# Hybrid attention and state-space layer: V's tiles on another queue, earlier stores, and a new order in the last head pair

## The chip, the cores and the metric

The kernel runs on one core of a Trainium2 chip. The core has a matrix engine (TensorE, "PE" in the profile; its weight loads are "PEld"), a vector engine (VectorE, DVE), a scalar engine (ScalarE, ACT), a general engine (GpSimd, POOL) and SyncE (SP), which here only issues transfers. Transfers (DMAs) are issued on the queues of SyncE, ScalarE or GpSimd and are carried out by 16 DMA engines that all queues share. Each engine works through its own instructions in order and waits on semaphores for the others. The metric is device time in microseconds (us), the median of several runs.

## The reference, cut to what matters

One decoder layer over a sequence of 2048 tokens of width 1024, all in float32. The input projection makes q, k, v and a gate z for attention, and the inputs of a state-space mixer. Attention has 16 heads of width 64. Every head attends three times, with dilations 1, 4 and 16 and a window of 128 steps, and the three results are mixed by a softmax over their log-sum-exps:

```python
o1, l1 = dilated_window_attention(q, k, v, slopes, DILATIONS[0])
o2, l2 = dilated_window_attention(q, k, v, slopes, DILATIONS[1])
o3, l3 = dilated_window_attention(q, k, v, slopes, DILATIONS[2])
wts = jax.nn.softmax(jnp.stack([l1, l2, l3], axis=0), axis=0)
y_att = wts[0][..., None] * o1 + wts[1][..., None] * o2 + wts[2][..., None] * o3
y_att = rms_norm(y_att.reshape(Bsz, S, D_ATT) * silu(z_att), att_norm_g)
# y_ssm: state-space scan over chunks of 128, gated and normed in the same way
mix = jnp.concatenate([y_att, y_ssm], axis=-1)
x = layer_norm(alpha * x + jnp.einsum('bse,ed->bsd', mix, w_out), ln_g, ln_b)
```

## The kernel before, in words

The kernel has three stages. The first (up to about 1148 us) projects the input and runs the state-space scan; it leaves q, k, V, the gates, the scan's output (`d_us`) and the output weights, split into high and low parts (`d_wo`), in device memory. The change does not touch it.

**Attention** (1148 to 1613 us) goes over 8 pairs of heads (`pr`), in each over the three windows (`d` = 0, 1, 2: dilations 16, 4, 1 in the order of the tables), four groups of blocks (`qd`) and two halves (`half`): 24 units to a pair, listed in `todo` (L1251). In step `i` of the loop (L1256) the scores and exponentials of unit `i` are issued, the transposes of unit `i - 2`, and the products with V (`values`, L990) of unit `i - 3`. Everything else hangs on the position `at` = (d, qd, half) of that last unit. `manual_schedule` (L1255) keeps the order of the program on each engine named; the order between engines comes from semaphores alone. The next block starts a new such region (L1343), and the instructions of the two regions are merged by the compiler's own time model, which may put the head of the second into the tail of the first.

A tile is taken from a ring of a given number of buffers (`bufs`). Whoever takes the next tile waits until the last use of the tile that had that buffer. The rings that matter: `v` and `vs` (V, and V shifted by half a block) with 3 buffers each, `wb` with 3, `num` with 6, `ex` with 3, and one `q` and one `k` for each of two pairs in turn. In the last pair the same buffers are taken for output weights (`big`, L1133; `load_w`, L1137) and for split blocks (`free`).

While pair `pr` is in attention, pair `pr - 1` is combined. `statistics` (L1036) transposes minima and sums (L1041) in two parts, after the second and the third window, and stores them; `gather` (L1058) reads them back in another layout; `weights` (L1063) makes the three mixing weights and stores them (`d_wd`, L1081); `broadcast` (L1083) reads each weight back, spread over the partitions, into a `wb` tile, by two transfers on SyncE (L1089). A memset of one element before it (L1087) makes VectorE, too, wait until the buffer is free (not for the first weight, and not in the last pair). `combine` (L1099) runs steps 0 to 5 on GpSimd: the first weight times its result (L1111), the second (L1111), their sum (L1115), the third (L1111), the sum (L1115), times the gate z (L1125). The result `u` is a `wb` tile too, and `keep_u` (L1095, L1096) stores it to `d_ua`. So a pair takes five `wb` tiles (three weights, z, u) out of three buffers, and the tile of a pair's third weight takes the buffer that held `u` of the pair before it.

SyncE's order within a pair, as the program gives it: gather, V and shifted V of window 2 (L888) at (0,0,0), tables, the weights' store, first broadcast at (0,3,0), `keep_u` at (1,0,0), the other broadcasts at (1,0,1) and (1,2,0), tables, z at (2,0,0). GpSimd issues the next pair's q, k, V of windows 0 and 1 and shifted V of window 1 between the steps of `combine`.

**The output projection** (from 1613 us) takes blocks of 128 tokens. For a block and a branch (`br` = 1 for the scan, 0 for attention) the raw input is fetched (`fetch_raw`, L1150), split into high and low parts (`split`, L1159: a cast on ScalarE, L1167, and a difference, L1169), squared and summed for its norm (`squares`, L1172), and multiplied with eight weight tiles in two halves (`product`, L1191; 24 matmuls each). `residual` (L1179) fetches rows of the input, `scaled` (L1183) scales them, `add` (L1215, L1218) adds a product to them, and `norm` (L1220) finishes and stores them. Products take accumulators out of six in turn, four of them named `S`. The first eight products are those of branch 1 for blocks 0 to 3, as branch 0 needs the last pair, whose weights, broadcasts and `combine` (here on VectorE) run beside them. In the block before the change SyncE is not among the engines whose order is kept (L1343), and the time model orders it.

## Time and profile before

| | |
|---|---|
| median of three timed runs | 2011.88 us (2008.34 to 2013.04) |
| the profiled execution's own time | 2003.82 us |
| span of the profile | 2002.0 us |
| mean granted TensorE clock | 0.991 |
| PE busy | 1945.7 us (97%) |
| DVE, ACT, POOL busy | 1275.8, 1120.0, 998.3 us |
| DMA | 447.67 MB, mean 224 GB/s |

The profile is one execution, and its times are microseconds from the start of the span. A row of the order in time gives start, length, engine, line of the kernel, operation, the tile written and the tiles read, and in brackets how long the engine stood idle before and what released it. "SPq" and "ACTq" are transfers being issued by SyncE and ScalarE; "x4" means that several like instructions are merged into one row. A row of the busy time in stretches gives the stretch, its length, and for each engine busy time and number of instructions, then granted clock (1.00 is full), the mean busy share of the DMA engines and GB/s. A busy TensorE is not always at its peak, since matmuls overlap. L-numbers are lines of the kernel before.

### The profile page before, as it was taken

What the parts mean: (1) busy time and instruction counts of PE and PEld (TensorE: products, weight loads), DVE (VectorE), ACT (ScalarE), POOL (GpSimd) and SP (SyncE); (2) the same over time, 40 slices, a digit from 0 to 9 for tenths busy, and PEclk for the clock granted to TensorE, in tenths of its full rate; (3) what the DMA queues carried; (4) which work ended last, traced back from release to release, by engine and by line L of the source; (5) the groups of instructions that cost most, each with busy time, mean ns of one, the idle gap of its engine ahead of it and who ended that gap; (6) DMA issues with size and microseconds to landing.
All of it is one profiled execution on the core that took longest, in us unless ns stands there. A gap on an engine that the chain in (4) does not pass through costs nothing.

```text
span 2002.0 us, 42714 instructions
## 1 busy us (share of the span) xinstructions
PE 1945.7 (97%) x16008; PEld 1588.2 (79%) x16008; DVE 1275.8 (64%) x3204; ACT 1120.0 (56%) x3036; POOL 998.3 (50%) x877
## 2 busy tenths in 40 slices
PE   8999999999999999999999999999999888999998
PEld 7888899888888888988888877777777666888886
DVE  7655376887766655644454388888887736655553
ACT  5454343566556774456566488988888732322220
POOL 0366514666556667155565343676776622432221
PEclk9999999999999999999999999999999998999999
DMA  6788676566787876888888766888888988332210
GB/s 270 236 284 293 213 280 227 159 195 190 237 306 266 279 245 239 312 269 256 272 277 259 256 228 165 229 244 235 252 238 254 265 242 260 134 102 92 92 61 32
DMA packets 260656, 447.67 MB, mean 224 GB/s; under 512 B 44785, under 2 KB 146673, under 8 KB 249057
## 3 DMA queue, kind: packets, MB, share of 16 engines
q1 hardware_dynamic: 170912, 205.39, 32.2%
q0 software_dynamic: 39088, 142.54, 21.6%
q10 hardware_dynamic: 50448, 97.01, 15.7%
q8 instruction: 126, 2.06, 0.4%
q14 instruction: 82, 0.66, 0.1%
HBM read 301.85 MB, written 151.39 MB: 226 GB/s over the span
## 4 chain that ended last, share of the span: by engine, by line
PE 85%; DVE 5%; DMA 4%; ACT 3%; issue 2%; POOL 1%; SPq 0%; ACTq 0%; DVEq 0%; POOLq 0%
PE pp L260 13%; PE pp L264 13%; PE pp L262 13%; PE N L1002 7%; PE S L947 6%; PE T L976 5%; PE pp L309 4%; PE S L1201 4%; PE S L1203 4%; PE S L1202 3%; PE ss L309 2%; PE T L1201 2%; PE T L1203 2%; PE T L1202 2%; PE ss L627 2%
## 5 line engine op out<-in xcount | busy, mean ns | idle before, releaser
L217 POOL TENSOR_TENSOR w<-wr,w 128x512 fp32r<-128x512 f32 x217 | 285.6, 1327 | 268.2 <-ACT w L216 184.0
L962 ACT ACTIVATE P<-P,st 128x192 f32<-128x192 f32 (+1 forms) x768 | 323.4, 423 | 59.9 <-DVE st L953 55.4
L252 ACT COPY ev<-pp 128x512 f32<-128x512 f32 x200 | 117.1, 587 | 315.3 <-PE pp L264 281.5
L953 DVE CUSTOM_DVE_ANT_0 P<-S,tb 128x192 f32<-128x192 f32 (+1 forms) x768 | 205.8, 324 | 53.6 <-PE S L947 44.1
L272 DVE TENSOR_TENSOR ev<-pp,ev 128x512 f32<-128x512 f32 x152 | 101.2, 686 | 140.6 <-PE pp L264 95.9
L216 ACT CAST w<-wr 128x512 fp32r<-128x512 f32 x224 | 134.1, 620 | 23.5 <-DVE wr L211 11.9
L962 ACT ACTIVATION_READ_ACCUMULATOR P<-P,st 128x1 f32 x768 | 145.0, 189 | 0.0
L1111 POOL TENSOR_TENSOR wb<-num,wb 128x2048 f32<-128x2048 f32 x21 | 95.7, 4558 | 93.7 <-DMA wb<-d_wd 90.2
L978 DVE COPY PT<-T 128x512 f32<-128x512 f32 x192 | 131.7, 686 | 3.8 <-PE T L976 3.8
L976 PE MATMUL T<-ident,P 128*128 128x128 f32 x768 | 127.3, 288 | 6.7 <-DVE PT L978 4.5
L1002 PE MATMUL N<-PT,v 128*64 128x64 f32 (+1 forms) x1536 | 124.5, 259 | 4.2 <-DVE PT L978 3.5
L976 PEld LDWEIGHTS T<-ident,P 128*128 128x128 f32 x768 | 81.3, 141 | 52.9 <-ACT P L962 16.8
L211 DVE TENSOR_TENSOR wr<-wr 128x512 f32<-128x512 f32 x128 | 112.2, 877 | 9.3 <-DMA wr<-w 5.9
L947 PE MATMUL S<-k,ex 64*64 64x192 f32 (+1 forms) x2048 | 108.8, 322 | 3.2 <-issue 3.2
L1002 PEld LDWEIGHTS N<-PT,v 128*64 128x64 f32 x1536 | 79.4, 138 | 38.3 <-issue 22.7
L459 DVE SCALAR_TENSOR_TENSOR ss<-U,cw,ss 128x512 f32<-128x512 f32 x144 | 106.0, 752 | 2.9 <-ACT ss L455 0.6
L1177 DVE TENSOR_REDUCE tb<-P 128x128 f32<-128x1024 f32 x30 | 60.2, 2006 | 45.1 <-ACT P L1174 21.1
L1239 POOL TENSOR_TENSOR k<-k,wb 128x1024 f32<-128x1024 f32 x8 | 25.8, 3225 | 122.0 <-DVE k L1238 122.0
L587 ACT ACTIVATE mt<-csb,wdr 128x128 f32<-128x128 f32 x256 | 78.9, 395 | 0.9 <-PE ss L627 0.8
L947 PEld LDWEIGHTS S<-k,ex 64*64 64x64 f32 x2048 | 66.4, 134 | 15.4 <-issue 8.9
L596 DVE TENSOR_TENSOR mt<-mt,ss 128x1024 f32<-128x1024 f32 x32 | 39.0, 1220 | 54.1 <-ACT mt L592 53.7
L260 PE MATMUL pp<-TT4h,w 128*128 128x512 f32 x176 | 69.6, 395 | 0.0
(493 smaller groups left out, 5991.1 us busy)
## 6 DMA issues: line engine op xcount, KB each, us to landing
wr<-w ACTq DMA_DIRECT2D x164, 256.0 KB
d_wc<-w SPq DMA_DIRECT2D x48, 512.0 KB
w<-d_wc POOLq DMA_DIRECT2D x48, 512.0 KB, 6.4
wb<-d_wd SPq DMA_DIRECT2D x48, 512.0 KB
d_wo<-wot POOLq DMA_DIRECT2D x32, 512.0 KB, 4.3
csb<-d_cs ACTq DMA_DIRECT2D x32, 512.0 KB
d_wv<-w SPq DMA_DIRECT2D x14, 1024.0 KB
w<-d_wv POOLq DMA_DIRECT2D x14, 1024.0 KB, 8.7
```

What stands on the lines that cost most here:

```text
L216: nc.scalar.copy(h, r)
L217: low.tensor_tensor(l, r, h.bitcast(F32), op=OP.subtract)
L260: nc.tensor.matmul(ps, w[:, 0, k], th[:, k], start=start and k == 0, stop=False, skip_group_check=not start)
L262: nc.tensor.matmul(ps, w[:, 0, k], tl[:, k], start=False, stop=False, skip_group_check=not start)
L264: nc.tensor.matmul(ps, w[:, 1, k], th[:, k], start=False, stop=(k == 3), skip_group_check=not start)
L309: nc.tensor.matmul(o, (th, tl)[j == 1][:, k, t], w[:, int(j == 2), k], start=start and r % 2 == k == j == 0, stop=(k == 3 and j == 2), ski ...
L947: nc.tensor.matmul(o, A["q"][d][64 * h:64 * h + 64, blk, 64 * a:64 * a + 64], kv, start=True, stop=True)
L953: nc.vector.tensor_tensor_reduce(P[:, h, cs], sp[h][:, cs], t, -0.125, 3.0e38, OP.add, OP.min, accum_out=stat(A, 0, d, h, blk))
L962: nc.scalar.activation(p, p, AF.Exp, bias=stat(A, 0, d, h, blk), scale=-1.0, accum_out=stat(A, 1, d, h, blk))
L976: nc.tensor.transpose(tp[:, h, i], P[:, h, 256 * i:256 * i + 128], ident)
L978: nc.vector.tensor_copy(pt, tp)
L1002: nc.tensor.matmul(o, l, r, start=start, stop=True, skip_group_check=True)
```

## The change

In attention, V of window 1 (`load_v(pairs[pr], "v", 1)`) and shifted V of window 1 go from GpSimd's queue to SyncE's, at (0,0,0) of their own pair and (2,0,1) of the pair before; V of window 2 moves from (0,0,0) to (0,1,1), shifted V of window 2 to (1,1,1), V of window 0 from (1,2,0) to (2,0,0). `keep_u` moves from (1,0,0) to (0,0,1). In pair 7 the raw inputs of blocks 0 and 1 are fetched at (1,0,1) instead of (1,2,0), and block 0 is split at (1,2,0) to (1,3,0) instead of (2,0,1) and (2,1,0); output weights are loaded at other positions, ahead of the step of `combine` at the same position, and partly into other tiles; z of pair 7 is fetched in attention, on SyncE. The third weight of pair 7 is broadcast into a tile of V's ring. In the output block SyncE's order is kept too; the broadcasts of pair 7 are issued before the residuals, which move from ScalarE's queue to SyncE's together with `keep_u` of pair 6; the third and later steps (split of block 3, `combine`, `add`) are put into another order.

```diff
@@ -1082,7 +1082,8 @@
 
         def broadcast(A, d):
 
-            wb = A["w", d] = cm_.tile([128, NR, NJ], F32, name="wb", bufs=3)
+            pool, name = (io, "v") if A["pr"] == 7 and d == 2 else (cm_, "wb")
+            wb = A["w", d] = pool.tile([128, NR, NJ], F32, name=name, bufs=3)
             if d and A["pr"] < 7:
                 nc.vector.memset(wb[:, 0, 0:1], 0.0)
             for h in range(2):
@@ -1105,8 +1106,6 @@
             pu = lambda a: a.rearrange("p (n r j) -> p r n j", r=NR, j=8)
             if k in (0, 1, 3):
                 d = k - k // 2
-                if last:
-                    broadcast(A, d)
                 wb = A["wb"] = A.pop(("w", d))
                 eng.tensor_tensor(wb, A["num"][d], wb, op=OP.mult)
                 if k == 0:
@@ -1178,7 +1177,7 @@
 
         def residual(n):
             o = O[n] = os_[n // 2][:, n % 2 * D:n % 2 * D + D] if n < 4 else O.pop(n - 4)
-            (nc.scalar if n < 4 else nc.sync).dma_start(o, xc[n * 128:(n + 1) * 128, :])
+            nc.sync.dma_start(o, xc[n * 128:(n + 1) * 128, :])
 
         def scaled(n):
             nc.scalar.activation(O[n], O[n], AF.Copy, scale=ALPHA)
@@ -1243,11 +1242,11 @@
         O = {}
         pairs = {}
         STEPS = {(1, 0, 0): (0, "q", 1),
-                 (1, 1, 0): (1, "k", 1), (1, 2, 0): (2, "v", 1, 0), (1, 3, 0): (3, None, 0), (2, 0, 0): (None, "v", 1, 1),
-                 (2, 1, 0): (4, "vs", 1, 1), (2, 2, 0): (5, None, 0)}
-        LOADS = {(1, 0, 0): ((8, None, "k_0"),), (1, 1, 0): ((9, None, "q_0"),), (1, 2, 0): ((11, None, "vs"),),
-                 (1, 3, 0): ((12, 0, "q_1"), (13, 0, "v")), (2, 1, 0): ((10, None, "ex"),),
-                 (2, 2, 0): ((14, 0, "v"), (15, 0, "vs"))}
+                 (1, 1, 0): (1, "k", 1), (1, 2, 0): (2, None, 0), (1, 3, 0): (3, None, 0), (2, 0, 0): (None, "v", 1, 0),
+                 (2, 1, 0): (4, None, 0), (2, 2, 0): (5, None, 0)}
+        LOADS = {(1, 0, 0): ((8, None, "k_0"),), (1, 1, 0): ((9, None, "q_0"),),
+                 (1, 3, 0): ((12, 0, "q_1"), (13, 0, "v")), (2, 0, 0): ((11, None, "num"), (14, 0, "v"), (15, 0, "vs")),
+                 (2, 1, 0): ((10, None, "ex"),)}
         todo = [(pr, d, qd, half) for pr in range(8) for d in range(3) for qd in range(4) for half in range(2)]
         pts = {}
         TA = 2
@@ -1300,24 +1299,45 @@
                     if at == (0, 0, 0) and pr < 7:
                         pairs[pr + 1] = load_pair(pr + 1)
                     if at == (0, 0, 0) and pr:
+                        load_v(pairs[pr], "v", 1, nc.sync)
+                    if at == (0, 1, 1) and pr:
                         load_v(pairs[pr], "v", 2, nc.sync)
-                        load_v(pairs[pr], "vs", 2, nc.sync)
                     if pr and at == (0, 2, 0):
                         load_tab(pairs[pr], 2)
-                    if pr > 1 and at == (1, 0, 0):
+                    if pr > 1 and at == (0, 0, 1):
                         keep_u(pairs[pr - 2], nc.sync)
                     if pr and at in ((0, 2, 0), (0, 2, 1), (0, 3, 0)):
                         weights(pairs[pr - 1], 2 * qd + half - 4)
                     if pr and at in ((0, 3, 0), (1, 0, 1), (1, 2, 0)):
                         broadcast(pairs[pr - 1], d + (at == (1, 2, 0)))
+                    if pr and at == (1, 1, 1):
+                        load_v(pairs[pr], "vs", 2, nc.sync)
                     if pr < 7 and at == (1, 1, 1):
                         load_tab(pairs[pr + 1], 0)
                     if pr and at == (2, 0, 0):
                         load_z(pairs[pr - 1])
-                    if pr == 7 and at in ((2, 0, 1), (2, 1, 0)):
-                        split(0, 1, slice(4 * qd, 4 * qd + 4), (0,))
-                    if pr == 7 and at == (2, 1, 0):
-                        split(0, 1, parts=(1,))
+                    if pr < 7 and at == (2, 0, 1):
+                        load_v(pairs[pr + 1], "vs", 1, nc.sync)
+                    if pr == 7:
+                        if at == (1, 0, 1):
+                            X = big("ex", F32)
+                            for j in range(2):
+                                fetch_raw(j, 1, X[:, j * D:j * D + D])
+                        if at == (1, 2, 0):
+                            free.append(big("vs"))
+                        if at == (2, 0, 0):
+                            zt7 = cm_.tile([128, NR, NJ], F32, name="num", bufs=6)
+                            nc.sync.dma_start(f2(zt7), d_za[7])
+                        for e, hf, name in LOADS.get(at, ()):
+                            load_w(e, hf, name)
+                        if at == (2, 0, 0):
+                            free.append(big("num"))
+                        if at in ((1, 2, 0), (1, 2, 1)):
+                            split(0, 1, slice(4 * half, 4 * half + 4), (0,))
+                        if at == (1, 3, 0):
+                            split(0, 1, parts=(1,))
+                        if at in ((2, 2, 1), (2, 3, 0)):
+                            fetch_raw(qd, 1)
                     if at in STEPS:
                         k, x, nx, *dd = STEPS[at]
                         if pr and k is not None:
@@ -1329,23 +1349,11 @@
                                 load_x(pairs[pr + nx], x)
                     if at == (2, 2, 0) and pr < 7:
                         permute(pairs[pr + 1], 1)
-                    if pr < 7:
-                        continue
-                    for e, hf, name in LOADS.get(at, ()):
-                        load_w(e, hf, name)
-                    if at == (2, 0, 0):
-                        zt7 = cm_.tile([128, NR, NJ], F32, name="num", bufs=6)
-                        free += [big("num"), big("num")]
-                    if at == (1, 2, 0):
-                        X = big("ex", F32)
-                        for j in range(2):
-                            fetch_raw(j, 1, X[:, j * D:j * D + D])
-        with tc.manual_schedule(engines={E.PE, E.DVE, E.Activation, E.Pool}):
+        with tc.manual_schedule(engines={E.PE, E.DVE, E.Activation, E.Pool, E.SP}):
             A = pairs[7]
             small = stp.tile([128, 192], F32, name="st")
             os_.append(X)
             free.append(big("ex"))
-            fetch_raw(2, 1)
             squares(0, 1)
             split(1, 1)
             squares(1, 1)
@@ -1362,16 +1370,10 @@
                 ps = product(n, br, hf)
                 adds.append((n, br, hf, ps))
                 if i == 2:
+                    combine(A, 0)
+                    load_w(0, 0, "num")
                     for j in range(2):
                         scaled(j)
-                    add(*adds.pop(0))
-                    add(*adds.pop(0))
-                    for j in range(3):
-                        combine(A, j)
-                    load_w(0, 0, "num")
-                    fetch_raw(3, 1)
-                    residual(2)
-                    residual(3)
                 if i > 4:
                     while adds:
                         add(*adds.pop(0))
@@ -1385,32 +1387,42 @@
                             weights(A, n)
                         os_.insert(0, big("k_1", F32))
                         for n in range(2):
+                            broadcast(A, n)
+                        for n in range(2):
                             residual(n)
+                        broadcast(A, 2)
+                        keep_u(pairs[6], nc.sync)
+                        for n in range(2, 4):
+                            residual(n)
+                    if i == 3:
+                        combine(A, 1)
+                        load_w(1, 0, "num")
+                        combine(A, 2)
                     squares(*ops[j])
-                    if i == 0:
-                        keep_u(pairs[6], nc.scalar)
-                        nc.scalar.dma_start(f2(zt7), d_za[7])
                     for m in (j + 2,) if 4 < j < 30 else ():
                         fetch_raw(*ops[m])
                     if j >= 7 and j + 1 < 32 and ops[j + 1][1]:
                         residual(ops[j + 1][0])
                         scaled(ops[j + 1][0])
                 if i == 3:
-                    fetch_raw(0, 0)
+                    add(*adds.pop(0))
+                    add(*adds.pop(0))
                     for j in range(2, 4):
                         scaled(j)
+                    load_w(2, 0, "vs")
+                    fetch_raw(0, 0)
                     for j in range(3, 6):
                         combine(A, j)
                         if j < 5:
                             add(*adds.pop(0))
                 if i == 4:
-                    for e, name in enumerate(("num", "vs", "v", "wb", "num", "wb", "num")):
-                        load_w(1 + e, 0, name)
+                    for e, name in enumerate(("wb", "wb", "num", "wb", "num")):
+                        load_w(3 + e, 0, name)
                         if e == 2:
                             fetch_raw(1, 0)
                     for e in range(8):
                         load_w(e, 1)
-                    lgb = big("wb", F32)
+                    lgb = f2(A["acc"])
                     lg, lb = lgb[:, 0:D], lgb[:, D:2 * D]
                     nc.sync.dma_start(lg, dap(lng, 0, [[0, 128], [1, D]]))
                     nc.sync.dma_start(lb, dap(lnb, 0, [[0, 128], [1, D]]))
```

## The prediction

> **What bounds the kernel now.** I read the page first, then the busy time in stretches of the attention stage, then the waits, and the order of time around the longest ones.
>
> ```profile
> span 2002.0 us, 42714 instructions
> PE 1945.7 (97%) x16008; PEld 1588.2 (79%) x16008; DVE 1275.8 (64%) x3204; ACT 1120.0 (56%) x3036; POOL 998.3 (50%) x877
> ```
>
> TensorE is busy for 97% of the span; only 56 us are open, so a change of order can win only where TensorE waits or runs at a lower clock. The change touches two places: attention, pair by pair, and the passage into the output projection. Cut at the second statistics transpose of each pair (T below), the busy time in stretches gives pairs 1 to 7, then parts of single pairs, then the passage. The first number is the length, then busy time of PE, PEld, DVE, ACT, POOL, granted clock, DMA share, GB/s.
>
> ```profile
> 1211.04:1265.90 54.86, 53.39 (x1032) 40.18 (x1027) 46.74 (x240) 48.23 (x217) 32.52 (x19) 1.00 0.76 216
> 1265.90:1319.25 53.35, 53.06 (x1032) 40.02 (x1026) 46.57 (x240) 48.15 (x217) 35.20 (x30) 1.00 0.86 244
> 1319.25:1375.75 56.50, 53.29 (x1033) 39.98 (x1026) 47.12 (x240) 48.24 (x217) 39.86 (x32) 1.00 0.85 240
> 1375.75:1432.85 57.10, 53.75 (x1034) 40.15 (x1027) 47.30 (x240) 48.59 (x220) 40.55 (x32) 1.00 0.85 243
> 1432.85:1489.50 56.65, 53.72 (x1032) 40.12 (x1026) 47.13 (x239) 47.82 (x215) 40.50 (x32) 1.00 0.87 245
> 1489.50:1547.18 57.68, 55.61 (x1032) 41.30 (x1027) 46.96 (x240) 48.18 (x217) 40.85 (x33) 0.97 0.84 238
> 1547.18:1613.10 65.92, 58.45 (x988) 42.81 (x982) 49.98 (x218) 47.94 (x201) 46.84 (x34) 0.92 0.87 254
> ...
> 1265.90:1299.94 34.04, 33.75 (x613) 24.78 (x608) 30.38 (x161) 31.34 (x145) 15.95 (x21) 1.00 0.85 220
> 1547.18:1583.54 36.36, 34.32 (x614) 24.90 (x608) 30.86 (x161) 31.63 (x146) 18.82 (x22) 1.00 0.83 212
> 1583.54:1613.10 29.56, 24.13 (x381) 17.92 (x375) 19.12 (x58) 16.30 (x56) 28.02 (x13) 0.83 0.93 306
> ...
> 1613.10:1647.11 34.01, 32.85 (x151) 26.49 (x145) 7.41 (x16) 10.45 (x15) 3.68 (x5) 1.00 0.90 247
> 1647.11:1659.55 12.44, 0.40 (x2) 0.00 (x0) 7.71 (x4) 0.02 (x1) 4.51 (x7) 0.69 1.15 247
> 1659.55:1665.30 5.75, 5.75 (x14) 4.50 (x15) 4.68 (x3) 2.94 (x3) 0.35 (x2) 0.50 1.21 400
> ```
>
> The same work takes 53.35 us in pair 2 and 56.5 to 57.7 in pairs 3 to 6. Pair 7 takes 65.92. Then TensorE stands still for 12 us, and its next 5.75 us run at half clock.
>
> **Part A: products stored sooner, V on SyncE (pairs 1 to 6).** What lengthens pairs 3 to 7 is a wait on VectorE (waits of the attention stage; two rows of pair 7 in order of time).
>
> ```profile
> DVE wb L1087 <- DMA d_ua<-wb: 9.4, 4, 2.6
> ...
> 1576.76 0.06 DVE L1087 MEMSET wb<- 128x1 f32 x1 [2.44 <-DMA d_ua<-wb]
> ...
> 1577.21 0.41 ACT L962 ACTIVATE P<-P,st 128x128 f32<-128x128 f32 x1 [2.75 <-DVE st L953]
> ```
>
> The memset that opens the third weight's tile (`wb`) must wait until the product of two pairs before has left that tile, and behind it on VectorE stand the next scores; ScalarE then idles 2.75 us. Why it leaves so late is in SyncE's order (pair 7, T = 1547.18), with the product on GpSimd that needs the first weight:
>
> ```profile
> 1554.95 0.54 SPq L888 DMA_DIRECT2D v<-d_v  x1
> 1555.58 2.49 SPq L888 DMA_DIRECT2D vs<-d_v  x1
> ...
> 1562.02 0.36 SPq L1081 DMA_DIRECT2D d_wd<-cm  x1
> 1565.68 1.12 SPq L1089 DMA_DIRECT2D wb<-d_wd  x2
> 1566.86 0.58 SPq L1096 DMA_DIRECT2D d_ua<-wb  x1
> 1567.49 10.45 SPq L1089 DMA_DIRECT2D wb<-d_wd  x4
> ...
> 1573.15 4.53 POOL L1111 TENSOR_TENSOR wb<-num,wb 128x2048 f32<-128x2048 f32 x1 [11.16 <-DMA wb<-d_wd]
> ```
>
> The store (L1096) stands behind the weights' store and the first broadcast. Moved to (0,0,1) it goes out near 1555.5, 11 us sooner, and the memset at 1576.8 finds the tile free. That removes about 2.4 us from each of pairs 3 to 7.
>
> Against it stands what SyncE gets in exchange. Ahead of the weights' store it now carries V, product, V instead of V and shifted V, and shifted V for the third window goes behind the second broadcast. Rates from the DMA queues, SyncE's own row in 1557:1561 (V and shifted V alone) and 1567:1571 (broadcast alone), then GpSimd's and SyncE's rows in 1584:1587 (both at once); packets, MB, share:
>
> ```profile
> q1 hardware_dynamic: 2512, 1.28, 109.6%
> ...
> q1 hardware_dynamic: 133, 0.96, 106.0%
> ...
> q0 software_dynamic: 87, 0.71, 79.3%
> q1 hardware_dynamic: 79, 0.17, 34.4%
> ```
>
> V moves at 1.28/4 = 0.32 MB/us, a broadcast at 0.24. The exchange adds 1.05 + 1.05 - 0.98 = 1.1 MB, 3.5 us; I take back 1 us because shifted V no longer moves while the statistics are gathered (bounds 0 and 2, no row has it). So the first weight lands 2.5 us later than now (1573.15, T + 26.0), at T + 28.5; the second 1.05/0.24 = 4.4 later, T + 32.9; shifted V 0.98/0.32 = 3.1 later, T + 36.0. It is first read one unit (2.4 us, 19.3/8 from the second part of pair 2, which is 53.35 - 34.04) after the first part: T + 34.0 + 2.4 = T + 36.4. It fits, by 0.4 us. The other V tiles have more room, but the first one for the next pair is put behind one more product on GpSimd:
>
> ```profile
> 1533.68 2.63 POOL L886 DMA_DIRECT2D v<-d_v  x4
> ```
>
> It is issued by 1536.3; the 4.5 of one product later is 1540.8, and a transfer of this size takes 7.5 from issue to use (1565.68 to 1573.15): it lands about 1 us after T of the next pair (1547.18), where its first readers come within one unit of 2.4. In a shorter pair that is tight too. I take 54.4 us for each of pairs 1 to 6, the 53.35 of pair 2 and one us of such waits (bounds 53.35 and 56.5). Pairs 3 to 6: 227.9 to 217.6; pairs 1 and 2: 108.2 to 108.8. **A = -9.7.**
>
> [...]
>
> **Part B: pair 7.** The first block's raw input is now asked for at (1,0,1), behind both broadcasts, and ScalarE's first cast of it stands at (1,2,0). That cast is due just before the exponentials quoted above, 1577.21 - 2.75 = 1574.5. The raw tile can't land before the second broadcast, T + 32.9 = 1580.1, and 0.8 us more (its first 0.26 MB at 0.32): ScalarE waits 6.4 us, with the next exponentials and the copies that free TensorE's accumulators behind it. I count 6 us for TensorE, and 2 for a lower clock after it (a wait of 3.2 us costs more below). Worse is possible: the first output weights (1 MB) now go ahead of the first product on GpSimd and meet V and the weights' store, and where both queues run they share by packets (87 to 79), so large packets push SyncE's small ones back, by up to 1.05/0.24 = 4.4 us. Better is possible if ScalarE has slack: none lost. First part: 34.0 + 8 = 42 for 36.4, +5.6 (bounds -2.4 and +11.6).
>
> [...]
>
> In the second part the split on GpSimd, which held TensorE, goes away:
>
> ```profile
> 1600.26 0.50 PE L1203 MATMUL S<-k,num 128*128 128x512 f32 x1 [3.23 <-POOL num L1169]
> ...
> 1600.26:1610.50 10.24, 8.75 (x90) 6.37 (x92) 8.54 (x8) 5.98 (x15) 10.22 (x4) 0.52 0.75 243
> ```
>
> That is 3.2 us and then 8.75 x 0.48 = 4.2 of clock. Reductions and the second block's split still fall in here, so of 7.4 I take 5.5 (bounds 2 and 9). **B = +5.6 - 5.5 = +0.1.**
>
> **Part C: the passage.** Now (SyncE's wait, then order of time on the engines):
>
> ```profile
> SPq L1089 <- DMA d_wd<-cm: 11.8, 2, 8.6
> ...
> 1624.60 0.38 SPq L1081 DMA_DIRECT2D d_wd<-cm  x1
> ...
> 1634.79 1.06 ACT L1184 ACTIVATE k<-k 128x1024 f32<-128x1024 f32 x1
> ...
> 1646.81 2.29 DVE L1111 TENSOR_TENSOR wb<-num,wb 128x2048 f32<-128x2048 f32 x1 [9.23 <-DMA wb<-d_wd]
> ...
> 1658.28 1.22 DVE L1169 TENSOR_TENSOR num<-P,num 128x1024 fp32r<-128x1024 f32 x1
> 1660.62 1.99 DVE L1177 TENSOR_REDUCE tb<-P 128x128 f32<-128x1024 f32 x1 [1.12 <-ACT P L1174]
> ...
> 1664.74 0.74 DVE L1218 SCALAR_TENSOR_TENSOR ex<-S,st,ex 128x512 f32<-128x512 f32 x1
> ```
>
> The weights' store takes 9.0 us until the broadcasts start (1624.60 plus 0.38 plus 8.6), because ScalarE's queue sends residuals, the product and z beside it; two products then stand ahead of the third block's split (L1169), for which TensorE waits. With ScalarE's queue empty I give the store 4.5 us (3.7 in pair 7 above, 1562.02 to 1565.68; 9 if the output weights on GpSimd alone do it): 1629.1. First weight 7.5 later, 1636.6; second 1641.0; two residuals, 1.05 MB at 0.32, 1644.3. ScalarE scales both before it casts the third block, three times about 1.0: 1647.3. Split 1.2, two more products' steps 4.6, reduction 2.0: 1655.1; the first add 0.7: 1655.8. That last step is what is late next: the split is done by 1648.5, but the seventh product needs an accumulator that only the first add frees, and that add has been moved behind the products. TensorE resumes at 1655.8 for 1659.55. The half clock stays. **C = -3.8** (bounds -9 and 0). After that the output weights arrive no later than TensorE asks, as now.
>
> **At nothing** I cost the rest: other tiles for output weights (they are asked for no later), z of pair 7 read during attention (1 MB less in the passage, already in C as an empty ScalarE queue), the third weight in V's ring (no wait for the product to leave), and SyncE's order written out to the end. The last hides here:
>
> ```profile
> 1673.35:2002.00 328.65, 318.93 (x1401) 258.49 (x1399) 179.10 (x242) 78.68 (x112) 89.33 (x36) 0.99 0.30 99
> ```
>
> The DMA engines are at 0.30, and a block's raw input is asked for two blocks ahead. If a store of output rows held SyncE for longer than that, each late load would cost its lateness.
>
> Sum: -9.7 + 0.1 - 3.8 = -13.4. The profiled run took 2003.8, so 1990.4; the three timed runs have a median of 2011.9, 8 us above that run, and I carry the difference over: **1998.5 us**. About 0.2% (4 us) is what a measurement of this kernel can tell from no change.
>
> **The rivals.**
> 1. *The last pair runs clean*: the raw input lands in time for the cast. For it: TensorE is up to two units ahead of ScalarE's due work. Against it: both broadcasts are ahead in one queue. B is 8 better: 1990.5. Chance 0.15.
> 2. *V waits replace the memset's wait*: shifted V or the first V comes 2 us late, pairs stay at 56. A is near 0, so -3.7: 2008.2, no change to tell. For it: 0.4 us of room. 0.14.
> 3. *Slower: shifted V behind the second broadcast.* Each us that it lands late holds TensorE that long in each of seven pairs; from 13.4/7 = 1.9 us late the change loses. At 3 us late it is +7.6, 2019.5, more with a lower clock, as pair 6 shows 0.97. For it: GpSimd's loads share by packets. Against it: the next load there starts only after the first product, 4.5 us past the first weight. 0.12.
> 4. *The passage doesn't change*, since the store stays at 9 us beside the output weights: C is 0, 2002.3. 0.09.
> The forecast has 0.50 and its own range is 1990 to 2007.
>
> **How the numbers follow.** Forecast, rival 1 and rival 4 are faster: 0.74. Same 0.14, slower 0.12. The range runs from 1988 (rival 1 and a little) to 2013, which leaves out rival 3 and the ends of others.
>
> **What would show it.** A: no row of L1087 waiting for d_ua, pairs 3 to 6 at 53.5 to 55; wrong if L1002 waits for V. B: a wait of ScalarE's L1167 for ex<-d_us near T + 27, and no wait of L1203 for GpSimd's L1169. C: L1089 less than 5 us after L1081, TensorE waiting for L1218 rather than L1169. The forecast falls if pairs 3 to 6 stay over 56 us.

## The result, and the profile after

The changed kernel takes 2021.5 us (median of 7 runs, 2016.1 to 2030.9), the kernel before beside it 2007.6 (7 runs). The ratio is 1.0074, with a 95% interval of 1.0048 to 1.0100: slower, where 1998.5 was forecast and 2013 was the end of the range. In the profiled execution the span went from 2002.0 to 2017.3 us, and TensorE is as busy in share as before:

```profile
span 2017.3 us, 42713 instructions
PE 1950.2 (97%) x16008; PEld 1592.5 (79%) x16008; DVE 1273.4 (63%) x3204; ACT 1118.9 (55%) x3036; POOL 980.6 (49%) x863
```

The busy time in stretches says where the 15.3 us are. Before the change: pairs 1 to 6 together, and the rest after the last statistics transpose (columns as in the prediction; the two parts of pair 7 stand there).

```profile
1211.04:1547.18 336.14, 322.81 (x6162) 241.75 (x6157) 281.83 (x1435) 289.21 (x1297) 229.48 (x173) 0.99 0.84 238
...
1613.11:2002.00 388.89, 365.96 (x1598) 296.02 (x1593) 205.79 (x272) 93.18 (x131) 101.42 (x53) 0.98 0.40 124
```

After: pairs 1 to 6, first and second part of pair 7, the rest.

```profile
1208.52:1557.10 348.58, 328.24 (x6163) 245.88 (x6157) 280.14 (x1435) 289.43 (x1297) 217.52 (x162) 0.98 0.83 232
1557.10:1602.57 45.47, 36.38 (x612) 26.71 (x607) 30.80 (x161) 32.67 (x148) 24.38 (x23) 0.89 0.85 237
1602.57:1635.41 32.84, 26.29 (x394) 20.14 (x391) 18.37 (x57) 15.03 (x53) 20.13 (x11) 0.84 0.72 235
1635.41:2017.30 381.89, 362.01 (x1584) 292.85 (x1579) 207.59 (x272) 93.77 (x131) 101.01 (x53) 0.98 0.38 122
```

Pairs 1 to 6 lost 12.4 us, pair 7 lost 9.1 and 3.3, the rest won 7.0, and the stage began 2.5 us sooner in this execution: +15.3. In pairs 1 to 6 TensorE's idle time grew by 7.0 us (13.3 to 20.3) and its busy time by 5.4, at a clock of 0.98 for 0.99. By pair the loss isn't where the stall was: pairs 1 and 2 took 59.4 and 57.9 us (54.9 and 53.4 before), pairs 3 to 6 57.3 to 58.5 (56.5 to 57.7 before). No single pair can be read closely, though: pair 1, in which no product is stored yet, took 54.9 us in e1 and 58.1 in e4, two runs below whose programs are alike in it.

TensorE's waits in pairs 1 to 6 (sum, times, longest), before:

```profile
PE T L976 <- DVE PT L978: 4.3, 3, 1.7
PE N L1002 <- DVE PT L978: 3.5, 3, 1.7
PE S L947 <- issue: 2.1, 3, 1.4
...
PE T L976 <- ACT P L962: 0.8, 1, 0.8
PE T L976 <- ACT num L1030: 0.8, 1, 0.8
```

and after:

```profile
PE N L1002 <- issue: 8.9, 7, 2.7
PE S L947 <- issue: 7.4, 5, 2.1
PE T L976 <- ACT P L962: 3.0, 2, 1.6
```

The waits for VectorE are gone but for 0.9 us of short ones. In their place stands "issue": time in which TensorE waited for nothing that the profile shows. That became the question of the experiments.

Not all of the waits for VectorE before the change stood behind the memset. Two pairs of rows, each VectorE's wait and the one of TensorE behind it:

```profile
1330.52 0.39 DVE L1069 TENSOR_TENSOR mm<-cm 128x32 f32<-128x32 f32 x1 [1.34 <-DMA cm<-d_st]
1333.06 0.68 PE L1002 MATMUL N<-PT,v 128*64 128x128 f32 x8 [1.69 <-DVE PT L978]
...
1406.63 0.06 DVE L1087 MEMSET wb<- 128x1 f32 x1 [2.42 <-DMA d_ua<-wb]
1408.56 0.63 PE L976 MATMUL T<-ident,P 128*128 128x128 f32 x4 [1.74 <-DVE PT L978]
```

The 3.5 us of L1002 stand behind VectorE's wait for the gathered statistics (L1069). Behind the memset stand the 4.3 us of L976, one wait in each of pairs 3 to 5; behind the memset of pair 6 (2.6 us at 1519.35) TensorE has no wait for VectorE; it had just waited 1.4 us put down to "issue". So VectorE's 2.4 us cost TensorE 1.2 to 1.7.

In pair 7 and the passage, ScalarE in order of time:

```profile
1593.89 0.62 ACT L1166 CAST vs<-ex 128x512 fp32r<-128x512 f32 x1 [9.73 <-DMA ex<-d_us]
...
1606.60 1.06 ACT L1173 ACTIVATE ex<-ex 128x1024 f32<-128x1024 f32 x1 [4.68 <-POOL vs L1168]
```

TensorE:

```profile
1596.47 0.48 PE L1002 MATMUL N<-PT,v 128*64 128x64 f32 x4 [9.09 <-ACT num L1030]
...
1608.68 0.69 PE L984 MATMUL T<-ident,P 128*128 128x128 f32 x2 [4.38 <-ACT sT L1046]
...
1626.03 0.44 PE L984 MATMUL T<-ident,P 128*128 128x128 f32 x2 [2.17 <-DVE PC L987]
...
1676.13 0.77 PE L1200 MATMUL S<-k,vs 128*128 128x512 f32 x1 [10.92 <-DVE k L1217]
```

SyncE:

```profile
1572.99 0.48 SPq L1081 DMA_DIRECT2D d_wd<-cm  x1
1580.11 2.41 SPq L1090 DMA_DIRECT2D wb<-d_wd  x4
1582.56 2.02 SPq L1154 DMA_DIRECT2D ex<-d_us  x4
...
1646.05 0.38 SPq L1081 DMA_DIRECT2D d_wd<-cm  x1
1650.41 3.17 SPq L1090 DMA_DIRECT2D wb<-d_wd  x4
1653.69 1.22 SPq L1180 DMA_DIRECT2D k<-xc  x2
```

GpSimd:

```profile
1587.43 4.49 POOL L1110 TENSOR_TENSOR wb<-num,wb 128x2048 f32<-128x2048 f32 x1 [15.20 <-DMA wb<-d_wd]
...
1604.22 2.35 POOL L1168 TENSOR_TENSOR vs<-ex,vs 128x1024 fp32r<-128x1024 f32 x1
```

ScalarE's cast waits 9.7 us for the raw input, and TensorE 9.1 behind it. Later ScalarE's squares (L1173) wait 4.7 us for the split on GpSimd (L1168), and TensorE 4.4 behind them. In the passage TensorE waits once, 10.9 us, for the first add (L1217) and no more for the split of block 3. Beside each of the four gaps in its rows its clock stands at 0.50, for 10.2, 6.8, 3.4 and 13.7 us in that order; the first of these two stretches holds such time and time at full clock:

```profile
1596.00:1608.00 12.00, 7.82 (x107) 5.82 (x107) 4.03 (x19) 6.23 (x24) 11.45 (x6) 0.64 1.07 286
...
1608.68:1612.00 3.32, 3.32 (x38) 2.49 (x38) 0.42 (x1) 1.83 (x8) 3.32 (x2) 0.50 0.10 17
```

### The profile page after: what moved, and what is told of

Its sections match the earlier page's. It is cut to its first block, busy times and chain, and to the rows that moved or that the text cites. A ratio compares the mean times of both kernels' runs of the same rounds, so it can differ in the third digit from the quotient of the medians.

```text
span 2017.3 us, 42713 instructions
## 1 busy us (share of the span) xinstructions
PE 1950.2 (97%) x16008; PEld 1592.5 (79%) x16008; DVE 1273.4 (63%) x3204; ACT 1118.9 (55%) x3036; POOL 980.6 (49%) x863
## 4 chain that ended last, share of the span: by engine, by line
PE 89%; DVE 3%; DMA 3%; ACT 2%; issue 2%; POOL 0%; SPq 0%; ACTq 0%; DVEq 0%; POOLq 0%
PE pp L260 14%; PE pp L264 14%; PE pp L262 14%; PE N L1002 8%; PE S L947 6%; PE T L976 5%; PE pp L309 4%; PE S L1200 4%; PE S L1201 4%; PE S L1202 4%; PE ss L309 2%; PE T L1200 2%; PE T L1201 2%; PE T L1202 2%; PE ss L627 2%
## 5 line engine op out<-in xcount | busy, mean ns | idle before, releaser
L1002 PE MATMUL N<-PT,v 128*64 128x64 f32 (+1 forms) x1536 | 125.2, 260 | 9.6 <-ACT num L1030 9.1
L976 PE MATMUL T<-ident,P 128*128 128x128 f32 x768 | 128.9, 291 | 3.0 <-ACT P L962 3.0
L976 PEld LDWEIGHTS T<-ident,P 128*128 128x128 f32 x768 | 82.4, 143 | 49.9 <-issue 18.8
L1002 PEld LDWEIGHTS N<-PT,v 128*64 128x64 f32 x1536 | 79.9, 139 | 43.4 <-issue 23.2
L1238 POOL TENSOR_TENSOR k<-k,v 128x1024 f32<-128x1024 f32 x8 | 25.8, 3220 | 122.5 <-DVE k L1237 122.5
L1176 DVE TENSOR_REDUCE tb<-P 128x128 f32<-128x1024 f32 x30 | 60.0, 1999 | 37.9 <-ACT P L1173 25.3
```

The source lines that it names most:

```text
L976: nc.tensor.transpose(tp[:, h, i], P[:, h, 256 * i:256 * i + 128], ident)
L1002: nc.tensor.matmul(o, l, r, start=start, stop=True, skip_group_check=True)
```

## The experiments

All runs in one table: ratio to the kernel before, timed beside it; length of pairs 1 to 6 in the profiled execution; TensorE's waits in them put down to "issue" and all others (some of the others turn out to be of the same kind, see "What 'issue' is"). Six pairs at the 53.35 us of pair 2 before would be 320.

| run | ratio (95% interval) | pairs 1-6 | issue | other |
|---|---|---|---|---|
| before | 1 | 336.1 | 2.6 | 10.5 |
| changed kernel | 1.0074 (1.0048 to 1.0100) | 348.6 | 16.3 | 3.9 |
| e1 sooner store alone | 1.0024 (1.0012 to 1.0036) | 349.9 | 15.4 | 2.1 |
| e2 V's moves alone | 1.0047 (1.0030 to 1.0064) | 355.4 | 6.4 | 15.8 |
| e4 changed, V back | 1.0070 (1.0055 to 1.0085) | 345.0 | 13.1 | 4.4 |
| e5 e4, early split back | 1.0049 (1.0031 to 1.0067) | 347.4 | 13.0 | 5.5 |
| e6 e1, broadcasts in 2 KB rows | 1.0065 (1.0048 to 1.0082) | 345.6 | 0.5 | 18.1 |
| e7 before, broadcasts in 2 KB rows | 1.0105 (1.0077 to 1.0133) | 353.9 | 1.2 | 21.5 |
| e8 before, 2 MB more, 8 KB rows | 1.0031 (1.0014 to 1.0049) | 344.8 | 8.1 | 10.8 |
| e9 before, 2 MB more, 2 KB rows | 1.0042 (1.0029 to 1.0056) | 351.5 | 12.3 | 11.0 |
| e10 e1, 3 MB less | 0.9976 (0.9961 to 0.9991) | 341.3 | 14.2 | 1.5 |
| e13 before, 3 MB less | 0.9931 (0.9905 to 0.9958) | 333.3 | 4.9 | 5.6 |
| e11 passage alone | 0.9981 (0.9967 to 0.9995) | 339.0 | 3.3 | 10.8 |
| e12 before without memset | 0.9985 (0.9975 to 0.9996) | 340.8 | 6.4 | 7.1 |
| e14 e1, third broadcast later | 1.0020 (1.0010 to 1.0029) | 347.9 | 17.5 | 3.3 |
| e15 e11 without memset | 0.9972 (0.9959 to 0.9985) | 342.4 | 9.8 | 8.1 |
| e16 e6, k ahead | 1.0031 (1.0012 to 1.0050) | 349.0 | 8.3 | 13.0 |
| e17 e16 with passage | 1.0009 (0.9997 to 1.0022) | 345.2 | 4.0 | 10.3 |
| e18 e17 in 4 KB rows | 0.9966 (0.9954 to 0.9978) | 340.3 | 7.4 | 7.0 |
| e19 e18, old store, no memset | 0.9960 (0.9947 to 0.9972) | 341.9 | 11.0 | 6.8 |

One profiled execution can stand a few us from the median of its kernel (e8's took 2008.5 us, its median is 2013.1); the ratio decides.

### Parts of the change (e1, e2, e4, e5)

The sooner store alone:

```diff
-                    if pr > 1 and at == (1, 0, 0):
+                    if pr > 1 and at == (0, 0, 1):
                         keep_u(pairs[pr - 2], nc.sync)
```

> The kernel before with one edit: the product's store (keep_u) at (0,0,1) instead of (1,0,0). Theory F (the loss in pairs 1 to 6 comes from V in SyncE's queue, which makes TensorE wait for its own instructions): the store alone removes the memset's wait of about 2.4 us in pairs 3 to 7, so 8 to 12 us faster than before, and the gaps of TensorE that the profile puts down to 'issue' stay as few as before (3.5 us in the waits of L947). Rival M (a TensorE that doesn't stop at the memset simply runs out of instructions later, whatever V does): within 2 us of before, with 'issue' gaps of 7 us or more in L947 and L1002. Rival L (V itself is late): as F, since V is untouched.

2011.6 us, 1.0024. The stall that the prediction wanted gone is gone, and the kernel is slower. Rival M comes nearest: "issue" takes 15.4 us in pairs 1 to 6, as in the changed kernel, with V untouched. Its time is missed: 4.6 us slower, where M had at most 2. Theory F, that V's place in SyncE's queue does it, falls.

V's moves alone (as in the change's diff, the store at its old place):

> The kernel before with V's five moves alone (V and shifted V of window 1 on SyncE, V of window 2 at (0,1,1), shifted V of window 2 at (1,1,1), V of window 0 at (2,0,0)); the product's store stays at (1,0,0). Theory F: pairs 1 and 2 lose 4 to 5 us each, as in the changed kernel, with gaps put down to 'issue'; pairs 3 to 6 keep the memset's wait and lose 3 or more each as well: 12 to 30 us slower than before. Rival L: the same sign, but then TensorE's L1002 waits for a DMA of v or vs in the profile. Rival M: within 4 us of before, because the memset's wait still covers it.

2018.8 us, 1.0047, slower as theory F and rival L had it; M, with at most 4 us, is missed again. Here shifted V did come late, which is rival L. TensorE's waits in pairs 1 to 6:

```profile
PE N L1002 <- DMA vs<-d_v: 12.6, 5, 3.0
PE N L1002 <- issue: 5.0, 4, 1.6
```

This is the prediction's third rival, at the 3 us it named, but only with the old store. In the changed kernel the store has left the place ahead of shifted V, and no row of L1002 waits for a DMA.

The changed kernel with V's moves undone:

> The changed kernel with V's five moves undone (sooner store, last pair and passage as changed). Theory F: pairs 1 to 6 take 53.5 to 55 us each, 12 + 10 us less than in the changed kernel; pair 7 still waits for the raw input, perhaps 3 us less as a MB less stands ahead of it: 1993 to 2003, which is 5 to 15 us faster than before. Rival M: pairs 1 to 6 stay at 57 to 58 us and the time at 2015 to 2021.

2022.3 us, 1.0070, just above what M had. V's moves are worth nothing in the changed kernel, which ends F a second time.

Then also the early split of block 0 undone:

```diff
-                        if at == (1, 0, 1):
+                        if at == (1, 2, 0):
                             X = big("ex", F32)
...
-                        if at in ((1, 2, 0), (1, 2, 1)):
-                            split(0, 1, slice(4 * half, 4 * half + 4), (0,))
-                        if at == (1, 3, 0):
+                        if at in ((2, 0, 1), (2, 1, 0)):
+                            split(0, 1, slice(4 * qd, 4 * qd + 4), (0,))
+                        if at == (2, 1, 0):
                             split(0, 1, parts=(1,))
```

> As the run with V's moves undone, and in the last pair the raw input is asked for at (1,2,0) and block 0 is split at (2,0,1) and (2,1,0), as before the change. Compared with that run it prices the early split. If the cast that waits for the raw input is what lengthens the first part of pair 7 (by 9.1 us in the changed kernel) and the split on GpSimd what holds the second part, the first part goes back to 34 to 37 us, the second stays at 29 to 33: 6 to 10 us faster than with the early split, about 1990 to 1995. If the first part stays over 42 us, the late first broadcast or the lower clock is the cause and the times agree within 3 us.

2017.3 us, 1.0049, far from the 1990 to 1995 that were expected. The parts of pair 7, with the early split (e4):

```profile
1555.56:1603.09 47.53, 36.11 (x614) 26.29 (x608) 31.10 (x161) 32.66 (x148) 26.79 (x25) 0.89 0.90 230
1603.09:1637.42 34.33, 27.23 (x396) 20.65 (x390) 18.32 (x57) 15.02 (x53) 20.59 (x11) 0.85 0.66 220
```

and without it (e5):

```profile
1557.16:1593.53 36.37, 34.08 (x614) 24.80 (x608) 30.96 (x161) 31.71 (x146) 16.15 (x22) 1.00 0.79 214
1593.53:1635.56 42.03, 28.73 (x397) 21.83 (x391) 19.14 (x58) 16.18 (x55) 31.74 (x14) 0.80 0.78 254
```

The cast costs the first part 11.2 us, as thought. But the second part then takes 42.0 us, not 29 to 33. SyncE and TensorE there:

```profile
1610.33 22.34 SPq L1154 DMA_DIRECT2D P<-d_us  x4
```

```profile
1616.61 0.80 PE L1202 MATMUL S<-k,vs 128*128 128x512 f32 x1 [6.34 <-POOL vs L1168]
...
1625.79 0.79 PE L1200 MATMUL S<-ex,vs 128*128 128x512 f32 x1 [4.09 <-DMA ex<-d_wo]
```

TensorE waits 6.3 us for the same split on GpSimd, and 4.1 for an output weight. SyncE spends 22 us over the raw inputs of blocks 2 and 3, which are asked for at (2,2,1) and (2,3,0), while exponentials still use their ring. The statistics' store stands behind them but isn't held: they are done at 1632.7, before its transpose at 1635.6.

### What "issue" is

Two queues of the trace carry instructions. One of them, q8, moves 126 packets of 16,384 bytes in the kernel before and in the changed one (the other has packets of 8,192 bytes and less). TensorE has 32,405 instruction records (matmuls, weight loads and 389 of its sequencer), which fits packets of 256 instructions (126 x 16,384 / 32,405 = 63.7 bytes each). In e1 SyncE's queue is alone for 8.2 us:

```profile
q1 hardware_dynamic: 526, 1.83, 105.3%
```

In the 1.5 us after that an instruction packet moves:

```profile
q1 hardware_dynamic: 36, 0.19, 63.5%
q0 software_dynamic: 12, 0.10, 30.6%
q8 instruction: 1, 0.02, 5.6%
q14 instruction: 1, 0.01, 3.0%
```

and then TensorE goes on:

```profile
1476.42 0.28 PE L1002 MATMUL N<-PC,vs 64*64 64x64 f32 x4 [3.26 <-issue]
```

This holds for all 125 gaps of TensorE of 0.7 us or more, between 1205 and 1605 us, that are put down to "issue" in the kernel before, the changed one and the eighteen of the experiments (e6 has none): each ends 2.2 to 3.1 us after the start of a q8 packet. The 108 such gaps with another releaser end anywhere from 0.1 to 10 us after one.

TensorE's own count says it more sharply. If its records are numbered in the order of their start, the last one before each of the 125 gaps is number 193 past a multiple of 256. Of the 108 others, 86 stand elsewhere, and 22 stand at number 193 too: these are most likely waits for instructions that the profile puts down to another engine. The two waits of L976 for ScalarE in the rows after the change are among them, as are the two in the rows before. Counted in this way, waits for instructions in pairs 1 to 6 went from 4.2 us (before) to 19.3 (changed), 16.9 in e1, and all other waits from 8.9 to 0.9, 0.6 in e1.

Counting gives the delay as well: outside attention a packet mostly starts when TensorE has run some 155 records past a multiple of 256. From there to number 193 of the next 256 are 294 records, an estimated 7.6 us at the pace of pair 2 (53.35 us for 2058 matmuls and weight loads). As 2.2 to 3.1 us pass between a packet's start and TensorE's going on, one that starts some 5 us behind that point would, by this estimate, leave TensorE dry; the packets behind the 125 gaps started 4.4 to 9.7 us behind it. The mean of this delay in us, in pairs 1 to 7, in their parts (a packet belongs to the part in which it starts), and outside (before 1148 us and after pair 7):

```
                          attention  first parts  second parts  outside
before                         3.72         3.54          3.98     1.92
changed kernel                 4.21         4.02          4.40     1.90
e1 sooner store                4.31         4.21          4.43     1.89
e6 e1, rows of 2 KB            3.05         2.22          4.43     1.82
e7 before, rows of 2 KB        2.54         2.37          2.76     1.86
e8 before, 2 MB more, 8 KB     4.22         3.88          4.71     1.84
e9 before, 2 MB more, 2 KB     4.64         4.10          5.39     1.82
e10 e1, 3 MB less              3.62         3.69          3.55     1.80
e13 before, 3 MB less          3.27         2.68          3.92     1.89
```

Packets start later in attention than outside it (before 3.72 us for 1.92, changed 4.21 for 1.90). The reading that fits is that TensorE there often stands close to the end of the instructions that it has, and runs dry when a packet starts late. Six runs change the traffic.

Broadcasts in rows of 2 KB, on top of the sooner store (e6) and on the kernel before (e7):

```diff
             for h in range(2):
-                nc.sync.dma_start(f2(wb[64 * h:64 * h + 64]), dap(d_wd[A["pr"]], (d * 2 + h) * S, [[0, 64], [1, S]]))
+                for c in range(0, S, 512):
+                    nc.sync.dma_start(f2(wb[64 * h:64 * h + 64])[:, c:c + 512],
+                                      dap(d_wd[A["pr"]], (d * 2 + h) * S + c, [[0, 64], [1, 512]]))
```

> The kernel with the sooner store alone, and each broadcast read in rows of 2 KB (four transfers of a quarter of the columns for one) instead of 8 KB; same bytes, same queue, same place. Theory P (TensorE's instructions come in packets of 16 KB over the same DMA engines, and packets of 8 KB of SyncE's queue keep such a packet waiting until TensorE runs dry): the gaps of TensorE that the profile puts down to 'issue' shrink below half of the 4 to 6 us a pair that they and their neighbours cost now, pairs 2 to 6 take 53.5 to 56 us instead of 58 to 60, and the time is 1992 to 2002. Rival S (it is the bytes in flight, not the size of a packet): no change against the sooner store alone, 2009 to 2014. Rival X (the gaps have nothing to do with the DMA engines): no change either, and no relation of gaps to instruction packets.

> The kernel before with the broadcasts in rows of 2 KB and nothing else. Theory P: the memset's wait of 2.4 us in pairs 3 to 7 stays, the 'issue' gaps of pairs 1, 6 and 7 go: 3 to 10 us faster than before, 1997 to 2004. Rivals S and X: within 2 us of before, or slower where eight transfers for two hold SyncE longer.

2021.7 us (1.0065) and 2029.7 (1.0105): the times went against theory P. The gaps did what it said: "issue" falls from 15.4 to 0.5 us (e6), the delay in first parts from 4.2 to 2.2, and pairs 1 to 6 win 4 us on e1 in the profiled execution, not the some 20 that the theory wanted of pairs 2 to 6. TensorE's longest waits there are now others:

```profile
PE S L947 <- DMA k<-d_k: 13.3, 5, 3.6
PE N L1002 <- DVE PT L978: 3.5, 3, 1.7
```

The sixteen transfers of two broadcasts hold SyncE for 11 to 13 us instead of 2.4 (in pairs 2 to 6), the weights land later, and GpSimd, which waits for them, asks for the next pair's k behind the second step. The rows are smaller and also spread over a longer time; these runs don't tell the two apart.

Two MB more in the third window, which nobody waits for, in rows of 8 KB (e8; e9 has rows of 2 KB, a quarter of the columns at a time):

```diff
+    d_xx = [dtile(f"d_xx{i}", [128, 2, S]) for i in range(8)]
...
                         load_z(pairs[pr - 1])
+                    if 0 < pr < 7 and at in ((2, 0, 1), (2, 1, 1)):
+                        for c in range(0, S, 2048):
+                            nc.sync.dma_start(dap(d_xx[pr], qd * S + c, [[2 * S, 128], [1, 2048]]),
+                                              dap(d_za[pr - 1], c, [[S, 128], [1, 2048]]))
```

> The kernel before with 2 MB more on SyncE in the third window of pairs 1 to 6 (two copies of 1 MB from device memory to device memory in rows of 8 KB at (2,0,1) and (2,1,1)), which no instruction waits for. Theory P: TensorE gets new 'issue' gaps in the third window, and each of pairs 1 to 6 takes 1.5 to 4 us more: 2016 to 2031. Rival X: TensorE waits for nothing that these copies delay, within 2 us of before. Rival S: as P.

> As the run with 2 MB more in rows of 8 KB, but the same bytes in rows of 2 KB. Theory P: most of the loss is gone, within 4 us of before. Rival S: as slow as with rows of 8 KB, 2016 to 2031. Rival X: within 2 us of before, as with rows of 8 KB.

2013.1 us (1.0031) and 2017.2 (1.0042). Rival X is out: transfers that nobody waits for cost time, and "issue" goes from 2.6 to 8.1 and 12.3 us, with packets later than before (3.7 to 4.2 and 4.6). Theory P had the signs but too much for 8 KB rows (2016 us or more). And rows of 2 KB were no better here, so the size of a row alone isn't the rule; this is what rival S had, though in e6 and e7 the delay fell with the bytes unchanged, which S doesn't explain.

Three MB a pair less, with the sooner store (e10) and on the kernel before (e13):

```diff
         def load_v(A, x, d, queue=nc.gpsimd):
 
+            if A["pr"] and (x, d) != ("v", 0) and (x, d) != ("vs", 1):
+                A[x][d] = A[x][0 if x == "v" else 1]
+                return
```

> The kernel with the sooner store alone, with V of windows 1 and 2 and shifted V of window 2 not loaded in pairs 1 to 7 (3 MB of the some 13 MB that a pair moves): the products of these windows read V of window 0 and shifted V of window 1 instead, so part of the attention's result is another one, with the same instructions on TensorE. Theory D (in attention the DMA engines are the bound: TensorE's own instruction packets are one of the things that come late behind other transfers, and with a stall taken away another transfer is late): the sooner store now keeps its gain, pairs 1 to 6 take 53.3 to 54.5 us each, gaps put down to 'issue' under 1 us a pair, 1975 to 1990. Rival X (TensorE's gaps have another cause than the DMA engines): pairs stay at 57 to 60 us, 2006 to 2014.

> The kernel before with the same 3 MB a pair left out (same remark on the result). Theory D: the memset's wait stays in part, since the first broadcast and the store behind it go out sooner too: pairs 3 to 6 take 53.5 to 56 us, 1978 to 1996, between 0 and 10 us slower than with the sooner store. Rival X: 2003 to 2011.

2002.3 us (0.9976) and 1993.7 (0.9931): 9.3 and 12.7 us less than the same kernels with the traffic. Less traffic helps, but less than theory D said: with the sooner store "issue" is still 14.2 us, though packets start no later on average (3.6 us) than in the kernel before (3.7). And the sooner store still loses, 8.5 us here.

### The memset, the store's place, and the passage (e11, e12, e14, e15)

The kernel before without the memset, store at its old place:

```diff
-            if d and A["pr"] < 7:
-                nc.vector.memset(wb[:, 0, 0:1], 0.0)
```

> The kernel before without the memset that opens the second and third weight's tile (L1087); the product's store stays at (1,0,0), so that the third broadcast's transfer itself, in SyncE's queue, waits until the product has left its buffer. Theory B (the sooner store loses because the three broadcasts, 3 MB in rows of 8 KB, then run without a break and hold TensorE's instruction packets back): here the store still stands between the first two broadcasts and the third still starts late, so the stall of VectorE goes and nothing comes in its place: pairs 3 to 6 take 54 to 56 us, 1996 to 2003. Theory K (any stall taken away is paid back, since TensorE only runs dry of instructions sooner): within 3 us of before, 2003 to 2010, or slower.

2004.1 us against 2008.1, 0.9985. The stall is worth about 3 us (interval 0.8 to 5.0), not 2.4 us in each of five pairs. Its profiled execution doesn't show where they were won: pairs 1 to 6 took 340.8 us in it, for 336.1 before. Of TensorE's waits for VectorE, those of L976 behind the memset (4.3 us) are gone; what is left stands behind the wait for the gathered statistics. "Issue" grows:

```profile
PE N L1002 <- DVE PT L978: 4.1, 3, 2.0
PE N L1002 <- issue: 3.7, 3, 1.9
PE S L947 <- issue: 2.7, 3, 1.3
```

The sooner store with the third broadcast at (1,3,0) instead of (1,2,0):

> The kernel with the sooner store alone, and the third broadcast at (1,3,0) instead of (1,2,0), some 5 us later. Theory B: the burst of broadcasts is broken, gaps put down to 'issue' near the start of the third window fall, pairs 2 to 6 take 55 to 57 us instead of 58 to 60, and the time is 1997 to 2005. Theory K: no change against the sooner store alone, 2008 to 2015.

2010.6 us, 1.0020: no change against e1. Theory B in this form falls, and theory K (what is taken away is paid back) stands: it had e12 at 2003 to 2010 us and allowed the 3.

The passage alone: the block after attention, `broadcast` and `residual` as in the changed kernel, attention as before, and

```diff
+            fetch_raw(2, 1)
+            fetch_raw(3, 1)
             squares(0, 1)
...
                         for n in range(2, 4):
                             residual(n)
+                        nc.sync.dma_start(f2(zt7), d_za[7])
```

> The kernel before with the passage of the changed kernel alone: attention in its old order (V, store, early raw input and split all as before), in the output block SyncE's order kept, broadcasts ahead of the residuals, the third broadcast in V's ring, residuals on SyncE, split of block 3 ahead of the second product; blocks 2 and 3 are fetched at the head of the block and z behind the residuals. If the passage's gain (some 7 us from the last statistics transpose to the end) stands by itself: 1998 to 2004, 3 to 9 us faster than before, and rest after that transpose 380 to 384 us. If the gain is only time that pair 7 lost before it: within 2 us of before.

2003.2 us, 0.9981 (0.9967 to 0.9995): faster than before, by 3 to 4 us. The rest takes 382.6 us, and the second part of pair 7 30.1, as before the change: the loss in pair 7 doesn't belong to the passage. Without the memset as well:

> The passage of the changed kernel alone (run before this one at 0.9981 of before), without the memset. The sum of the two: by theory B 1992 to 1999, by theory K 1999 to 2007.

2002.1 us, 0.9972, what theory K had for the two together (1999 to 2007).

### Repairs (e16 to e19)

k ahead of the second step, broadcasts in 2 KB rows (pair 7's in 8 KB):

```diff
                         k, x, nx, *dd = STEPS[at]
+                        if x == "k" and 0 < pr < 7:
+                            load_x(pairs[pr + nx], x)
                         if pr and k is not None:
                             combine(pairs[pr - 1], k)
...
-                            else:
+                            elif x == "q" or not pr:
                                 load_x(pairs[pr + nx], x)
```

> As the run with the sooner store and broadcasts in rows of 2 KB, with two edits: the next pair's k is asked for on GpSimd ahead of the second step of the combination instead of behind it (4.5 us sooner), and the broadcasts of the last pair, in the passage, stay in rows of 8 KB. Theory P2 (rows of 2 KB let TensorE's instructions through, and what they gained in the first two windows was lost because the slower broadcasts hold GpSimd, and so k, by up to 3.6 us a pair): the waits for k go, no gaps put down to 'issue' come back, pairs 2 to 6 take 54 to 57 us, 2003 to 2010, 5 to 14 us faster than without the two edits. Theory K (what is taken away comes back elsewhere): pairs stay at 57 to 61 us, 2010 to 2022.

> The same with the passage of the changed kernel. The passage was worth 4 us by itself: by theory P2 1997 to 2006, by theory K 2005 to 2018.

> The same with broadcasts in rows of 4 KB: half the transfers on SyncE, so the weights land sooner than with 2 KB. If the delay of an instruction packet goes with the size of the rows, 'issue' gaps come back in part (up to half of the 3 us a pair with 8 KB), 1998 to 2008; if any row below 8 KB is as good, it is 2 to 5 us faster than with 2 KB.

> The last kernel (passage, rows of 4 KB, k ahead) with the product's store at its old place (1,0,0) and without the memset. It prices the store's place where instruction packets are delayed less. If the old place is better by itself, as the run without the memset was 7.5 us faster than the one with the sooner store: 1993 to 1998. If that difference came from rows of 8 KB running without a break, it is gone with rows of 4 KB: 1998 to 2004.

2014.3 (1.0031), 2010.1 (1.0009), 2000.3 (0.9966) and 2001.9 (0.9960, against a 2010.3 beside it). The wait for k went, and the two edits of e16 together win some 7 us on e6, as theory P2 had it; but the time stays above the 2010 us it allowed, and "issue" came back in part. Rows of 4 KB are some 10 us better than rows of 2 KB: 2000.3 us is inside what was expected if the delay goes with the size of the rows (1998 to 2008), and above the 2 to 5 us expected if any row below 8 KB is as good. Whether the sooner weights or something else brings the 10 us was not taken apart. With 4 KB rows the new place of the store, and the old place without the memset, give the same within the intervals. e18 and e19 beat both kernels, by 0.34% and 0.40% of the kernel before.

## Why the prediction was wrong

**A, the step that failed: "That removes about 2.4 us from each of pairs 3 to 7."** The wait of the memset is gone, the store goes out where it was put, and no V is late in pairs 1 to 6, all as worked out. A came out at +12.4 for -9.7 even so, for two reasons.

VectorE's 2.4 us were not TensorE's. Behind them TensorE lost 4.3 us in pairs 3 to 5 together and nothing in pair 6, so the memset's wait had not much over 4 us to give. e12, which takes this wait away without moving anything, wins about 3 us.

And the stall sat on top of another limit, which the prediction didn't price: the packets of q8, read as TensorE's own instructions. Where TensorE doesn't stop for VectorE it would use its instructions up sooner, and stop for the next packet. That its stops go with these packets is shown (125 gaps at one place of its count, each ending 2.2 to 3.1 us after a packet's start); that it stops for want of one, and that the missing stall is what brings it there, is the reading that fits e1, e10 and e12. In pairs 1 to 6 of the changed kernel waits other than "issue" fell by 6.6 us and "issue" rose by 13.7, and 5.4 us of busy time came on top. Nearly all of that is clock: it is at half for 3.4 us four times in these pairs (from 1250.9, 1356.7, 1476.2 and 1527.4 us, each beside an "issue" wait of 1.4 to 2.7 us) and once before, and half of the 10.2 us more is 5.1. What could have warned were a DMA share of 0.84 to 0.87 in pairs 2 to 6, which the prediction shows, and "issue" waits of up to 1.4 us already before, which it doesn't.

Why the sooner store loses at all, and doesn't win the 3 us of e12, is not settled. With rows of 8 KB it loses 4.6 us (e1), 8.5 us with 3 MB less (e10 against e13), and no less with the third broadcast later (e14); with rows of 4 KB it does as well as the old place without the memset (e18, e19).

**Rivals 2 and 3** priced a lateness of V. It is real (e2), at the size worked out for rival 3, and the sooner store is what kept it out of the changed kernel. The kernel was slower for another reason; V's moves add nothing to it (e4).

**B, +12.4 for +0.1.** The first half was right in its mechanism: the cast waits for raw input behind both broadcasts. It was under-sized, 9.1 us for 5.6 and inside its bounds: pair 7's weights' store took 7.1 us (1572.99 to 1580.11) beside an output weight, not 3.7, so the first weight was used at T + 30.3 instead of T + 28.5 and the raw input at T + 36.8 instead of T + 33.7. The second half failed at "the split on GpSimd, which held TensorE, goes away". On GpSimd the early split stands behind the first product, the second and their sum; these came late with the weights, so that the split ran at 1604.2, and ScalarE's squares of the same block, which the compiler's time model had put ahead of exponentials, waited for it. TensorE stood 4.4 us and ran at 0.50 after it: +3.3 for -5.5.

**C, right, and larger than forecast.** The weights' store takes 4.0 us until the broadcasts (1646.05 plus 0.38 to 1650.41; forecast 4.5), TensorE waits for the first add and not for the split, and resumes 40.7 us after the transpose for 46.4 before: 5.7 us sooner, forecast 3.8. The whole rest won 7.0. By itself the passage is worth 3 to 4 us of the kernel's time (e11).

**At nothing** were put the other tiles for output weights, as "asked for no later"; the sooner raw inputs of blocks 2 and 3 weren't mentioned. At least one of the two is not nothing: in e5, which keeps both, TensorE waits 4.1 us for an output weight, SyncE is held for 22, and the second part of pair 7 takes 42.0 us; with the old positions it takes 30.1 (e11). No run prices them one by one.

**The base.** The forecast started from the three runs' 2011.9 us. Seven runs gave 2007.6, so the same sum would have given 1994.2: the miss is that of the sum, -13.4 for +13.9.

## What to carry to other kernels

Where, as here, the DMA engines are some 85% busy (0.84 to 0.87 in pairs 2 to 6) and TensorE 97%, a stall is not yet a gain to be had: price it by TensorE's own wait behind it, look at what "issue" waits say, and at the queue of instruction packets, and ask how far the engine's instructions reach when the stall is gone. Take the stall away with the smallest edit first (here two lines, worth about 3 us) and move transfers only afterwards. An instruction that is moved ahead in an order that is kept can carry its wait to what stands behind it: the cast on ScalarE (it waited 9.7 us, TensorE 9.1 behind it), the raw inputs on SyncE (22.3 us in e5) and the split on GpSimd (TensorE stood 4.4 us) each did that here.
